# A first transfer to 16 partitions, and a later first store, in an RMSNorm with swish

## The chip, the core and the metric

The kernel runs on one core of one Trainium2 chip. Its metric is the device time of one execution in microseconds (us), as the median of a few runs.

## What is computed

`x` has 16 x 1024 rows of 512 fp32 values. Each row is divided by its root mean square, multiplied by `gamma`, and put through swish.

```python
rms = np.sqrt(np.mean(x ** 2, axis=-1, keepdims=True) + eps)
x_norm = x / rms * gamma
return (x_norm * (1.0 / (1.0 + np.exp(-x_norm)))).astype(np.float32)
```

So 33.55 MB are read from HBM and 33.55 MB are written to it, and each value is touched a handful of times in between.

## The kernel before

**Layout.** The 16,384 rows of `x` are cut into four groups of 4,096. In a group, partition p of SBUF holds 32 rows that lie one after another in memory (64 KB). A "row" below is one such row on all 128 partitions, 256 KB. The SBUF buffer `xb` is a ring of 96 rows: group 0 in rows 0 to 31, group 1 in 32 to 63, group 2 in 64 to 95, and group 3 again in 0 to 31 (`slots`, L29). Everything is done in place in `xb`.

**Loads** (`loads`, L30 to L32) are triples of group, first row and count, all issued by SyncE (SP) on one DMA queue, q1, in the order of the list: 4, 4, 8, 8 and 8 rows of group 0, 16 and 16 of group 1, 24 and 8 of group 2, 24 and 8 of group 3. Each one is a single DMA of 128 runs, one per partition. The first two (`early = 2`, L38) are moved into the preamble of the program. Only the loads of group 3 have to wait: they overwrite group 0, so SP waits (L127) until the stores of those rows have landed. Each load has a semaphore, `ld[i]`.

**Compute** goes in 18 chunks (`units`, L36): 4, 4, then 14 times 8, then 4 and 4 rows. For chunk k:

- `square(k)`, ScalarE (ACT): waits for the load that begins with this chunk (L166), then squares and sums some rows with an accumulator (L168), and squares the rest into `sq` (L176).
- `sums(k)`, VectorE (DVE): sums `sq` over the row (L225) and adds eps (L232).
- GpSimd (POOL) raises to the power -0.5 (L153).
- `norm(k)`, DVE: x times rstd times gamma, one instruction per row (L243).
- `swish(k)`, ACT: Silu over the chunk (L188), two chunks behind `square`.

`gamma` arrives by a small DMA on ACT's queue (L206), behind another small one (L202), and is spread to all partitions by one shuffle on DVE (L256), ahead of the first `norm`.

**Stores** (`stores`, L33 and L34) are issued by ACT on its own DMA queue, q10: 24 and 8 rows of group 0, 32 of group 1, 16 and 16 of group 2, and 16, 8, 8 of group 3. `hold` (L35) delays two of them: store 0 (24 rows of group 0) is issued at chunk 7 at the earliest, and ACT waits (L196) until the load of rows 0 to 23 of group 2 has landed; store 2 waits in the same way for rows 0 to 23 of group 3. ACT runs its instructions in order, so what stands behind such a wait waits with it. The order on ACT around store 0 is: `square(7)`, the wait for the load, store 0, store 1, `swish(5)`, `square(8)`, `swish(6)`.

At the end SP waits for the stores that it has not waited for yet (L265).

Of the kernel before, what the change touches and what calls it, by code (L numbers as in the profile page):

```python
# [9 lines left out]
def kernel(  # L10
# [7 lines left out]
    nc = tc.nc  # L18
    P = nc.NUM_PARTITIONS
# [4 lines left out]
    xf = x.flatten_outer_dims()  # L24
# [2 lines left out]

    groups = [32] * 4
    slots = [0, 32, 64, 0]  # L29
    loads = [(0, 0, 4), (0, 4, 4), (0, 8, 8), (0, 16, 8), (0, 24, 8)]  # L30
    loads += [(1, 0, 16), (1, 16, 16)]
    loads += [(2, 0, 24), (2, 24, 8), (3, 0, 24), (3, 24, 8)]  # L32
    stores = [(0, 0, 24), (0, 24, 8), (1, 0, 32), (2, 0, 16), (2, 16, 16)]  # L33
    stores += [(3, 0, 16), (3, 16, 8), (3, 24, 8)]  # L34
    hold = {0: (loads.index((2, 0, 24)), 7), 2: (loads.index((3, 0, 24)), 12)}  # L35
    behind = {}  # L36
    units = [4, 4] + [8] * 14 + [4, 4]
    ring = 96  # L38
    early = 2
# [3 lines left out]
    assert P * sum(groups) == R, R  # L43
    assert all(s + n <= ring for s, n in zip(slots, groups))

    chunks, row = [], 0
    for n in units:
        g = max(g for g in range(len(groups)) if first[g] <= row)
        r = row - first[g]
        i = next(i for i, (h, q, m) in enumerate(loads) if h == g and q <= r < q + m)  # L50
        assert r + n <= loads[i][1] + loads[i][2]
        chunks.append((slots[g] + r, row, n, i if r == loads[i][1] else None))
        row += n
    K = len(chunks)
    rows = row
    assert rows * P == R
# [29 lines left out]
    ld = [nc.alloc_semaphore(f"ld{t}") for t in range(len(loads))]  # L86
# [16 lines left out]
    def need(ins, sem, value):  # L103
        return ins.wait_op(sem, value, "sem-ge")

    def dram(ap, piece):
        g, r, n = piece
        rows = ap[P * first[g] : P * (first[g] + groups[g])]
        return rows.rearrange("(p n) d -> p n d", n=groups[g])[:, r : r + n, :]

    def place(piece):
        g, r, n = piece
        return slots[g] + r, slots[g] + r + n

    def buf(piece):
        a, b = place(piece)
        return xb[:, a:b, :]

    stored_by_sync = set()

    def load(i):
        a, b = place(loads[i])
        for u, piece in enumerate(stores):
            c, d = place(piece)
            over = piece[0] < loads[i][0] and c < b and a < d
            if (over or behind.get(i) == u) and u not in stored_by_sync:
                nc.sync.wait_ge(st[u], 16)  # L127
                stored_by_sync.add(u)
        return nc.sync.dma_start(
            out=buf(loads[i]), in_=dram(xf, loads[i])  # L130
        ).then_inc(ld[i], 16)

    entry = nc.main_func.blocks[0].instructions
# [1 line left out]
    for t in range(early):  # L135
        ins = load(t).ins
        assert here[-1] is ins or here[-1].name == ins.name
        here.pop()
        at = next(
            i for i, other in enumerate(entry)  # L140
            if other.engine == mybir.EngineType.SP
            and isinstance(other, mybir.InstDrain)
        )
        entry.insert(at, ins)
    for t in range(early, len(loads)):
        load(t)
# [4 lines left out]
    for k, (_, row, n, _) in enumerate(chunks):  # L151
        need(
            nc.gpsimd.tensor_tensor(  # L153
                out=rstd[:, row : row + n], in0=ms[:, row : row + n],
# [7 lines left out]
    def square(k):  # L162
        nonlocal n_acc
        at, row, n, landing = chunks[k]
        if landing is not None:
            nc.scalar.wait_ge(ld[landing], 16)  # L166
        for j in range(n_sq[n], n):
            acc = nc.scalar.activation(  # L168
                out=junk[n_acc % 2], in_=xb[:, at + j, :], func=AF.Square,
                scale=inv_d**0.5, accum_out=ms[:, row + j : row + j + 1],  # L170
            )
            if n_acc >= 2:
                need(acc, s_acc, n_acc - 1)
            acc.then_inc(s_acc, 1)
            n_acc += 1
        square = nc.scalar.activation(  # L176
            out=sq[k % 2][:, : n_sq[n], :], in_=xb[:, at : at + n_sq[n], :],
            func=AF.Square, scale=inv_d**0.5,
        )
        if k >= 2:  # L180
            need(square, s_sum, k - 1)
        square.then_inc(s_sq, 1)

    def swish(k):
        at, _, n, _ = chunks[k]
        block = xb[:, at : at + n, :]
        need(
            nc.scalar.activation(out=block, in_=block, func=AF.Silu), s_norm, k + 1  # L188
        ).then_inc(s_swish, 1)
# [20 lines left out]
    stored = 0  # L210
    for k in range(K + 3):
        if k < K:
            square(k)
        while stored < len(stores) and max(ends[stored] + 2, after(stored)) <= k:
            store(stored)
            stored += 1
        if 2 <= k < K + 2:
            swish(k - 2)
# [3 lines left out]
    def sums(k):  # L222
        _, row, n, _ = chunks[k]
        need(
            nc.vector.tensor_reduce(  # L225
                out=ms[:, row : row + n_sq[n]], in_=sq[k % 2][:, : n_sq[n], :],
                op=ALU.add, axis=mybir.AxisListType.X,
            ),
            s_sq, k + 1,
        ).then_inc(s_sum, 1)  # L230
        need(
            nc.vector.tensor_scalar(  # L232
                out=ms[:, row : row + n], in0=ms[:, row : row + n],
                scalar1=eps_f, scalar2=None, op0=ALU.add,
            ),
            s_sum, k + 1,
        ).then_inc(s_eps, 1)
# [12 lines left out]

    for k in range(K + 1):
        if k < K:
            sums(k)
# [47 lines left out]
```

## Time and profile before

| | |
|---|---|
| median of 3 runs | 160.8 us (160.52 to 160.92) |
| the profiled execution, its own time | 160.12 us |
| span of its trace | 158.8 us |
| DVE busy | 131.6 us, 83% of the span |
| ACT busy | 125.0 us, 79% |
| POOL busy | 35.1 us, 22% |
| moved by DMA | 67.14 MB, mean 423 GB/s |
| first square on ACT starts | 4.92 us |
| DVE gets gamma, shuffle starts | 13.06 us |
| stores 0 and 1 issued | from 56.53 us |
| last store issued | 146.25 us |

The profile describes one execution. Its own time is 1.32 us above the span of its trace, and 0.68 us below the median of the runs. Busy times of engines leave out the issuing of DMAs; the row DMA of the page gives the share of time in which the 16 DMA engines were busy, in 40 equal slices of the span.

### The profile page before, as it was taken

Reading aid. Unit: us, or ns where it says so; the run is one execution under the profiler, and the core shown is the slowest. Engines: PE = TensorE matmul, PEld = TensorE weight load, DVE = VectorE, ACT = ScalarE, POOL = GpSimd, SP = SyncE. Lnnn points to the kernel's source line nnn. Section 1 sums busy time; section 2 is a strip of 40 time slices with the busy share of each in tenths; the row PEclk is TensorE's granted clock in tenths of the full one; section 3 lists DMA queues with packets and bytes.
Section 4 is the critical chain, followed back from the end, with each engine's and each line's share of the span. In section 5 each row is a group of like instructions: output and inputs, shape, how many; then the busy total and the mean of one; then the engine's idle time right before and its main releaser. Section 6 shows DMA issues by size and latency. Waiting matters only on the chain.

```text
span 158.8 us, 403 instructions
## 1 busy us (share of the span) xinstructions
DVE 131.6 (83%) x167; ACT 125.0 (79%) x137; POOL 35.1 (22%) x24
## 2 busy tenths in 40 slices
DVE  0117989999999999999999999999999999993000
ACT  0949699499898979998989898989898939786000
POOL 1021152213040505050505050504031323030000
DMA  7999999999999799999999989989979999999997
GB/s 281 443 415 446 421 499 404 396 470 448 404 433 522 305 363 491 396 409 400 417 491 409 458 388 429 561 380 413 528 305 454 429 421 429 454 413 437 400 437 310
DMA packets 2890, 67.14 MB, mean 423 GB/s; under 512 B 452, under 2 KB 452, under 8 KB 456
## 3 DMA queue, kind: packets, MB, share of 16 engines
q1 hardware_dynamic: 1584, 33.56, 50.0%
q10 hardware_dynamic: 1304, 33.57, 49.0%
q14 instruction: 2, 0.02, 0.0%
HBM read 33.56 MB, written 33.56 MB: 423 GB/s over the span
## 4 chain that ended last, share of the span: by engine, by line
DVE 68%; ACT 11%; DMA 7%; issue 4%; ACTq 1%; POOL 0%; another core or an unknown queue 0%; POOLq 0%
DVE xb L243 45%; DVE ms L225 21%; DMA gamma<-in_gamma_dram 7%; ACT sq L176 4%; ACT junk L168 4%; ACT xb L188 4%; DVE ms L232 1%; ACTq L198 0%; DVE gamma_sb L256 0%; POOL gamma L150 0%; POOL blank L149 0%; ACTq L196 0%; POOLq L68 0%
## 5 line engine op out<-in xcount | busy, mean ns | idle before, releaser
L243 DVE SCALAR_TENSOR_TENSOR xb<-xb,rstd,gamma_sb 128x512 f32<-128x512 f32 x128 | 86.2, 746 | 0.0
L188 ACT ACTIVATE xb<-xb 128x4096 f32<-128x4096 f32 (+1 forms) x18 | 58.3, 3236 | 14.8 <-DVE xb L243 14.8
L153 POOL TENSOR_TENSOR rstd<-ms,neg_half 128x8 f32<-128x8 f32 (+1 forms) x18 | 34.3, 1907 | 103.7 <-DVE ms L232 103.7
L225 DVE TENSOR_REDUCE ms<-sq 128x5 f32<-128x2560 f32 (+1 forms) x18 | 44.3, 2462 | 5.7 <-ACT sq L176 5.6
L176 ACT ACTIVATE sq<-xb 128x2560 f32<-128x2560 f32 (+1 forms) x18 | 36.3, 2019 | 0.0
L168 ACT ACTIVATE junk<-xb 128x512 f32<-128x512 f32 x50 | 29.1, 581 | 2.8 <-DMA xb<-in_x_dram 2.6
L168 ACT ACTIVATION_READ_ACCUMULATOR junk<-xb 128x1 f32 x50 | 9.3, 186 | 0.0
L209 ACT ACT_TABLE_LOAD x1 | 1.3, 1283 | 3.6 <-issue 3.6
L256 DVE LOAD_MASK_SELECT gamma_sb<-gamma x1 | 0.0, 14 | 4.4 <-DMA gamma<-in_gamma_dram 4.4
L232 DVE TENSOR_SCALAR ms<-ms 128x8 f32<-128x8 f32 (+1 forms) x18 | 3.1, 171 | 0.6
L220 DVE MEMSET neg_half<- 128x8 f32 x1 | 0.1, 65 | 2.0 <-PEq L68 2.0
L256 DVE STREAM_SHUFFLE gamma_sb<-gamma 128x512 f32<-128x512 f32 x1 | 0.7, 719 | 0.0
L150 POOL MEMSET gamma<- 128x512 f32 x1 | 0.5, 524 | 0.0
L149 POOL MEMSET blank<- 128x16 f32 x1 | 0.1, 111 | 1.5 <-POOLq L68 1.5
L282 POOL MEMSET const-float32-0.0<- 128x1 f32 x1 | 0.1, 98 | 0.2 <-issue 0.2
L282 POOL MEMSET const-bfloat16-1.0<- 128x1 bf16 x1 | 0.1, 101 | 0.0
L282 POOL MEMSET const-uint8-127<- 128x1 uint8 x1 | 0.1, 101 | 0.0
L282 POOL MEMSET const-float32-1.0<- 128x1 f32 x1 | 0.1, 98 | 0.0
## 6 DMA issues: line engine op xcount, KB each, us to landing
xb<-in_x_dram SPq DMA_DIRECT2D x2, 6144.0 KB, 35.7
out_dram<-xb ACTq DMA_DIRECT2D x3, 4096.0 KB, 20.5
xb<-in_x_dram SPq DMA_DIRECT2D x5, 2048.0 KB, 19.1
xb<-in_x_dram SPq DMA_DIRECT2D x2, 4096.0 KB, 33.0
out_dram<-xb ACTq DMA_DIRECT2D x1, 6144.0 KB, 19.9
out_dram<-xb ACTq DMA_DIRECT2D x3, 2048.0 KB, 12.6
xb<-in_x_dram SPq DMA_DIRECT2D x2, 1024.0 KB, 5.6
scratch<-blank ACTq DMA_DIRECT2D x1, 8.0 KB, 9.7
```

Source lines behind the costliest of these rows:

```text
L149: nc.gpsimd.memset(blank, 0.0).then_inc(s_blank, 1)
L150: nc.gpsimd.memset(gamma4, 0.0).then_inc(s_zero, 1)
L153: nc.gpsimd.tensor_tensor(out=rstd[:, row : row + n], in0=ms[:, row : row + n], in1=neg_half[:, :n], op=ALU.pow,),
L168: acc = nc.scalar.activation(out=junk[n_acc % 2], in_=xb[:, at + j, :], func=AF.Square, scale=inv_d**0.5, accum_out=ms[:, row + j : row + ...
L176: square = nc.scalar.activation(out=sq[k % 2][:, : n_sq[n], :], in_=xb[:, at : at + n_sq[n], :], func=AF.Square, scale=inv_d**0.5,)
L188: nc.scalar.activation(out=block, in_=block, func=AF.Silu), s_norm, k + 1
L209: nc.scalar.preload_act_table_set("silu_and_others")
L225: nc.vector.tensor_reduce(out=ms[:, row : row + n_sq[n]], in_=sq[k % 2][:, : n_sq[n], :], op=ALU.add, axis=mybir.AxisListType.X,),
L232: nc.vector.tensor_scalar(out=ms[:, row : row + n], in0=ms[:, row : row + n], scalar1=eps_f, scalar2=None, op0=ALU.add,),
L243: ins = nc.vector.scalar_tensor_tensor(out=x_row, in0=x_row, scalar=rstd[:, row + j : row + j + 1], in1=gamma_sb, op0=ALU.mult, op1=ALU.mult,)
L256: nc.vector.stream_shuffle(gamma_sb, gamma4, [0] * 32), s_gld, 16
L282: nc = _bacc.Bacc("TRN2", target_bir_lowering=False, num_devices=1)
```

## The change

Two things change. First, the loads of rows 0 to 15 of group 0. Before, they were three DMAs over all 128 partitions (4, 4 and 8 rows). Now a new first DMA loads all 16 rows of partitions 0 to 15 (16 runs of 32 KB), and the three old ones leave those partitions out and carry partitions 16 to 127 (112 runs each). The two DMAs in the preamble are now the 16-partition one and the first of the three. A chunk may now need more than one load, so `chunks` holds a list and `square` waits for each load in it; the first chunk waits for two.

Second, group 2 is loaded as 27 and 5 rows (was 24 and 8), and store 0 waits for the 27. What is left to load when store 0 may go is then 5 rows (was 8).

The order of instructions on DVE, ACT and POOL is the same as before, apart from the added wait of ACT. SP issues 12 loads (were 11).

```diff
-    loads = [(0, 0, 4), (0, 4, 4), (0, 8, 8), (0, 16, 8), (0, 24, 8)]
-    loads += [(1, 0, 16), (1, 16, 16)]
-    loads += [(2, 0, 24), (2, 24, 8), (3, 0, 24), (3, 24, 8)]
+    loads = [(0, 0, 16), (0, 0, 4), (0, 4, 4), (0, 8, 8), (0, 16, 8), (0, 24, 8)]
+    loads += [(1, 0, 16), (1, 16, 16), (2, 0, 27), (2, 27, 5)]
+    loads += [(3, 0, 24), (3, 24, 8)]
...
-    hold = {0: (loads.index((2, 0, 24)), 7), 2: (loads.index((3, 0, 24)), 12)}
+    hold = {0: (loads.index((2, 0, 27)), 7), 2: (loads.index((3, 0, 24)), 12)}
     behind = {}
+    narrow = {0: (0, 16), 1: (16, P), 2: (16, P), 3: (16, P)}
...
+    parts = [(0, P)] * len(loads)
+    for i, p in narrow.items():
+        parts[i] = p
...
+        need_now = [
+            i for i, (h, q, m) in enumerate(loads)
+            if h == g and q < r + n and r < q + m and i not in awaited
+        ]
+        awaited.update(need_now)
+        chunks.append((slots[g] + r, row, n, need_now))
...
     def load(i):
+        p, q = parts[i]
...
-            out=buf(loads[i]), in_=dram(xf, loads[i])
+            out=buf(loads[i])[p:q], in_=dram(xf, loads[i])[p:q]
...
-        if landing is not None:
-            nc.scalar.wait_ge(ld[landing], 16)
+        for i in landing:
+            nc.scalar.wait_ge(ld[i], 16)
```

## The prediction

> **What bounds the kernel now.** I read the page first: the busy shares, the slices, the DMA queues.
>
> ```profile
> DVE 131.6 (83%) x167; ACT 125.0 (79%) x137; POOL 35.1 (22%) x24
> ...
> DMA  7999999999999799999999989989979999999997
> GB/s 281 443 415 446 421 499 404 396 470 448 404 433 522 305 363 491 396 409 400 417 491 409 458 388 429 561 380 413 528 305 454 429 421 429 454 413 437 400 437 310
> DMA packets 2890, 67.14 MB, mean 423 GB/s; under 512 B 452, under 2 KB 452, under 8 KB 456
> ...
> q1 hardware_dynamic: 1584, 33.56, 50.0%
> q10 hardware_dynamic: 1304, 33.57, 49.0%
> ```
>
> DVE has the largest busy share of the compute engines, and the chain of waits runs mostly through it. But it stops in slice 37 of 40, while DMA is full from the first slice to the last: loads (q1) and stores (q10) take 50.0% + 49.0% of 16 engines' time. The DMA engines are the bound. What lengthens their work, or idles them, is paid in full; what moves compute is free while stores are issued in time.
>
> The trace's packet records give the DMA sum. One run on one partition is one packet; 16 packets are in flight at any time, and a 128-run DMA gives each engine 8. A packet of 8 KB takes 309 ns, 16 KB 611, 32 KB 1,213, 48 KB 1,815, 64 KB 2,418. Per engine that is 16 x 0.309 + 64 x 0.611 + 40 x 1.213 + 24 x 1.815 + 8 x 2.418 = 155.5 us. The engines' first packets start at 1.01 to 1.52 us, and the last one ends at 158.4: some 1.7 us are lost on the way. The busy times by stretch show where.
>
> ```profile
> 1.00:4.00 3.00, 0.07 (x1) 0.38 (x1) 0.57 (x2) 1.00 0.96 371
> ...
> 55.00:57.00 2.00, 2.00 (x4) 1.28 (x1) 0.00 (x0) 1.00 1.02 434
> 57.00:60.40 3.40, 3.37 (x4) 2.99 (x1) 0.59 (x1) 1.00 1.03 308
> ...
> 95.00:99.00 4.00, 4.00 (x6) 3.42 (x4) 0.00 (x0) 1.00 1.01 430
> ```
>
> The last two numbers are DMA share and GB/s. The engines are "busy" from 57.0 to 60.4 us, yet move 308 GB/s, not 430: 3.40 x (1 - 308/430) = 0.96 us is lost, with 16 KB packets of up to 1.28 us. This lies between the issue of stores 0 and 1 (56.53 us) and their first packet (60.38 us in the records). Around store 2 (issued 95.89) nothing is lost. So there are two places to win, the start and this stretch, and the change touches both.
>
> **Part 1, rows 0 to 15.** Before, per engine: 8 x (0.309 + 0.309 + 0.611) = 9.83 us. After, if the packets are spread evenly and run at the speeds above: 1 x 1.213 + 7 x 1.229 = 9.81. One more DMA costs SP one issue (0.4 us, the rows of 0.00 and 0.42 us); SP has issued all it may by 5.42 us, and the next load's data are due tens of us later, so that is hidden. The first chunk waits for two loads, 1.4 MB instead of 1.0; that is also hidden, since DVE sits until 13.06 us for gamma and ACT for 2.62 us for the third load.
>
> What the trace doesn't show is a large DMA into 16 partitions only. All 16 packets of the new first DMA go there at once. Lower bound: each runs at the 32 KB row, 1.213 us. Upper bound: in the trace a partition never gets more, over a load, than its share, 430 / 128 = 3.36 GB/s; if 16 neighbours can't take more than 16 shares, 32,768 B / 3.36 = 9.75 us, with all engines behind them. The only small case, gamma's four packets of 2 KB (81 to 84 ns), were spread over partitions 0, 32, 64, 96 and did not meet. No row is near; I take the middle, 5.5 us: **+4.3 us** (ends 0 and +8.5). For the three 112-run DMAs the bounds are 7 x 1.229 = 8.60 (engines) and 9.83 (as slow as with 128 partitions); I take 9.2: **+0.6** (ends 0 and +1.2).
>
> The Trainium skill (SBUF — State Buffer, "Door 1: The DMA port swizzle") speaks against the change: a DMA reaches memory through 16 ports, partitions 0 to 15 lie behind four of them, and 1 MiB to these partitions was measured at 104 GB/s. By that figure 512 KB would take an estimated 5.0 us, 3.8 above the packet row instead of my 4.3, and the sum below would give 164.6 us. By the packet row alone it would cost nothing. No run shown here has such a transfer, and the records of before can't decide: their 16 streams are spread over all 128 partitions.
>
> At the start there is something to gain: engines begin over 0.51 us (1.01 to 1.52), and first packets of 8 KB take up to 0.71 us. With 16 runs to describe instead of 128 all could begin together. Between 0 and 0.5 I take **-0.25**.
>
> **Part 2, store 0 waits for 27 rows.** A row takes 8 x 1.815 / 24 = 0.605 us, so the awaited load lands 3 x 0.605 = 1.8 us later. The timeline around the wait:
>
> ```profile
> 53.96 2.32 ACT L176 ACTIVATE sq<-xb 128x2560 f32<-128x2560 f32 x1
> 56.53 0.83 ACTq L198 DMA_DIRECT2D out_dram<-xb  x2
> ...
> 57.41 3.62 ACT L188 ACTIVATE xb<-xb 128x4096 f32<-128x4096 f32 x1 [1.13 <-DVE xb L243]
> ...
> 62.77 2.28 ACT L176 ACTIVATE sq<-xb 128x2560 f32<-128x2560 f32 x1
> ...
> 65.08 2.83 DVE L225 TENSOR_REDUCE ms<-sq 128x5 f32<-128x2560 f32 x1
> ```
>
> ACT is done at 56.28 and now waits only some 0.2 us. After, it waits about 1.8 us longer, with stores 0 and 1, `swish(5)` and `square(8)` queued behind. DVE's L225 starts within 0.03 us of the end of that square, so DVE, busy to the end from here, moves 1.8 us too. The stores it feeds are early enough: store 5 is issued at 134.71 and its first packet runs at 139.01, store 7 at 146.25 and 153.5. Cost **0** in this part; if that cover is gone, 1.3 us (rival D).
>
> DMA: with 5 rows left, 5 x 0.605 = 3.0 us of loads remain, less some 0.4 between last packet and landing. A store needs at least the 1.01 us that the first load took from issue to packet, so q1 still covers it. The gain lies in the slow stretch: none if it has nothing to do with the stores (as around store 2), all 0.96 if it is their issue beside many loads. I take a third, **-0.3**, since one of two such places shows it and 5 of 8 rows remain.
>
> **Sum.** +4.3 + 0.6 - 0.25 - 0.3 = +4.35. On the profiled execution: 160.12 + 4.35 = 164.5. The median of the runs lies 0.68 higher, so **165.1 us**. Compute goes along: if the loads come 4.6 us later and ACT's wait another 1.8, the last store is issued at about 152.5, and its turn on the engines comes at 153.5 + 4.35 = 157.9.
>
> **The rivals.**
> A, the forecast, 0.61: the 16 partitions can't take 16 streams at full speed. For: no row shows a partition range taking more than its share. Own range: from packets at half speed, 2.4 us (+1.2 - 0.55, 161.5) to all ends at once (9.7 - 0.25, 170.3).
> B, 0.27, not slower: the engines alone limit, as every packet row has it (27 GB/s per engine whatever the size). Then part 1 is -0.25 and part 2 about half of 0.96, together -0.75: 160.05, with 159.3 (both gains in full) to 160.6. It decides if the first 32 KB packets take under 1.5 us.
> C, 0.07: the spread is not what the change wants: the 16 packets go to the few engines that otherwise serve these partitions. Then those take 9.8 us for it and skip the next three DMAs, and each engine's total is as before: 160.8, 160.4 to 161.1. The first chunk would start after 10 us, hidden by gamma.
> D, 0.05: the start is like B, but the moved compute reaches the DMA. Store 5 would be issued at 136.5. If the 3.5 to 3.9 us from issue to first packet (stores 2 and 0) are needed in a busy queue too, its data start at 140.2, while store 4 is drained at about 138.8: +1.3 after the gains, 161.9. It decides if a store's first packet comes over 3 us after its issue with its queue empty.
>
> The Trainium skill (DMA: Bandwidth & Descriptors, "Why a DMA increments its semaphore by 16 and not by 1") speaks against C: the number of engines is the largest up to 16 that divides the outer sizes, and both 16 and 112 give 16. Nothing in the trace shows it for these shapes.
>
> **How the numbers follow.** About 0.3% (0.5 us) is what can be told from no change here. A and D are slower: 0.66. C and the upper end of B (0.03) are within 0.3%: 0.10. The rest of B is faster: 0.24. The range starts at 160.0, which leaves out the lower half of B (0.13), and ends at 169.5, which leaves out the last of A (0.04); A alone is 161.5 to 170.3.
>
> **What would show it.** Right: from 1 to 6 us the DMA moves 110 to 250 GB/s while "busy", the first packets are 32 KB of 3 us or more, and ACT's first square starts at 8 us or later (4.92 before); the awaited load lands past 62 us. Wrong: 420 GB/s from the second us on, 32 KB packets of 1.2 us. For part 2: ACT idle for some 1.8 us ahead of store 0, and GB/s between store 0's issue and its first packet; 430 there means the stretch was curable, 308 that it moved along. An idle slice of DMA near 139 us would speak for D.

## The result and the profile after

The changed kernel takes 168.42 us (median of 5, 167.50 to 168.74) against 160.69 us of the kernel before in the same comparison (160.05 to 160.92): a ratio of 1.0477, 95% interval 1.045 to 1.0504, so 7.7 us slower. The forecast was 165.1 us, slower. The profiled execution took 168.42 us with a span of 167.1.

The page of the changed kernel, the lines that answer to those of before:

```profile
DVE 131.7 (79%) x167; ACT 124.9 (75%) x137; POOL 35.1 (21%) x24
...
DMA  8899999998999997999899899999998999999995
GB/s 127 192 310 304 318 435 451 400 478 377 480 480 452 437 424 308 447 529 400 357 510 388 376 447 392 463 455 392 424 471 361 431 424 431 447 416 447 400 435 255
DMA packets 2874, 67.14 MB, mean 402 GB/s; under 512 B 468, under 2 KB 468, under 8 KB 472
```

The compute engines do the same work, and the DMA engines are still busy: the row DMA stands at 7 to 9 in every slice but the last. But in the first five slices (20.9 us) the row GB/s stands at 127 to 318 where it stood at 281 to 446. "Busy" is not "moving": the time is lost inside the packets. The busy times by stretch set a border to it. The last column is GB/s; the bytes of a packet are counted where it starts. First the kernel before:

```profile
4.00:8.00 4.00, 0.80 (x1) 3.87 (x9) 0.00 (x0) 1.00 1.06 440
8.00:12.00 4.00, 0.59 (x2) 1.56 (x4) 1.01 (x1) 1.00 1.00 424
12.00:16.00 4.00, 2.91 (x6) 3.82 (x7) 0.84 (x1) 1.00 1.01 434
```

Then the changed kernel:

```profile
1.00:4.00 3.00, 0.07 (x1) 0.39 (x1) 0.57 (x2) 1.00 1.20 175
4.00:8.00 4.00, 0.00 (x0) 0.89 (x1) 0.00 (x0) 1.00 0.85 184
8.00:12.00 4.00, 0.00 (x0) 1.92 (x5) 0.00 (x0) 1.00 1.03 293
12.00:16.00 4.00, 1.77 (x4) 2.60 (x6) 1.01 (x1) 1.00 1.06 310
16.00:20.00 4.00, 3.96 (x7) 0.00 (x0) 1.47 (x1) 1.00 0.93 274
20.00:57.00 37.00, 32.76 (x38) 33.29 (x40) 8.28 (x4) 1.00 1.03 444
57.00:60.40 3.40, 3.37 (x7) 3.40 (x8) 2.07 (x1) 1.00 1.02 439
60.40:64.00 3.60, 3.60 (x6) 2.19 (x1) 0.00 (x0) 1.00 0.78 338
64.00:68.00 4.00, 3.97 (x6) 1.19 (x1) 1.88 (x1) 1.00 1.17 497
```

Where 424 to 440 GB/s stood from 4 to 16 us, there are 184 to 310. The loss ends at 20 us, when rows 0 to 15 have landed (19.94 us). Everything behind comes later than before, so the place to look for the slow stretch of before is not 57.0 to 60.4 us, but ahead of this kernel's own first store, which is issued at 65.94 us and has its first packet at 67.36. The last two lines make 422 GB/s together, and the packet records show 0.04 us lost there: the stretch is gone.

The packet records give the terms. "Undisturbed" is the time that a packet of its size takes almost everywhere else in the traces, as listed in the prediction. Per engine, rows 0 to 15 took 10.12 us before. After, the one packet of 32 KB took 3.61 us on the mean (3.00 to 3.99, undisturbed 1.213), the 14 packets of 8 KB 7.13 us in all (0.510 each, undisturbed 0.309) and the 7 of 16 KB 6.50 us (0.928 each, undisturbed 0.611): 17.24, which is **7.1 us more**. The following load lost another 0.3.

ACT saw it at once. The timeline of the changed kernel, where the first square and the first store are issued:

```profile
10.08 0.60 ACT L178 ACTIVATE junk<-xb 128x512 f32<-128x512 f32 x1 [5.19 <-DMA xb<-in_x_dram]
...
60.27 2.32 ACT L186 ACTIVATE sq<-xb 128x2560 f32<-128x2560 f32 x1
65.94 0.82 ACTq L208 DMA_DIRECT2D out_dram<-xb  x2
66.81 3.62 ACT L198 ACTIVATE xb<-xb 128x4096 f32<-128x4096 f32 x1 [4.22 <-DMA xb<-in_x_dram]
```

The first square starts at 10.08 us (4.92 before). ACT is done at 62.59 and stands still until the 27 rows have landed and store 0 goes, at 65.94.

### The profile page after: what moved, and what is told of

The parts are those of the page before. It is cut to its first block, busy times and chain, and to the rows that moved or that the text cites. A ratio compares the mean times of both kernels' runs of the same rounds, so it can differ in the third digit from the quotient of the medians.

```text
span 167.1 us, 405 instructions
## 1 busy us (share of the span) xinstructions
DVE 131.7 (79%) x167; ACT 124.9 (75%) x137; POOL 35.1 (21%) x24
## 4 chain that ended last, share of the span: by engine, by line
DVE 62%; ACT 13%; DMA 11%; issue 3%; another core or an unknown queue 2%; ACTq 0%; SPq 0%
DVE xb L253 41%; DVE ms L235 20%; DMA xb<-in_x_dram 11%; ACT sq L186 5%; ACT junk L178 5%; ACT xb L198 4%; DVE ms L242 1%; ACTq L208 0%; SPq L139 0%; ACTq L206 0%; ACTq L176 0%
## 6 DMA issues: line engine op xcount, KB each, us to landing
out_dram<-xb ACTq DMA_DIRECT2D x3, 4096.0 KB, 19.4
xb<-in_x_dram SPq DMA_DIRECT2D x1, 6144.0 KB, 19.4
```

## Experiments

The theory after this: the loads of rows 0 to 15 cost 7 us because of the set of partitions they go to, and the wait for 27 rows is free. The rivals: the wait is paid by what stands behind it on ACT; the start of a program or the memory side, not the partitions, makes the first DMA slow.

### Each part by itself

Part 1 alone:

```diff
-    loads += [(1, 0, 16), (1, 16, 16), (2, 0, 27), (2, 27, 5)]
+    loads += [(1, 0, 16), (1, 16, 16), (2, 0, 24), (2, 24, 8)]
...
-    hold = {0: (loads.index((2, 0, 27)), 7), 2: (loads.index((3, 0, 24)), 12)}
+    hold = {0: (loads.index((2, 0, 24)), 7), 2: (loads.index((3, 0, 24)), 12)}
```

> Part 1 alone: the 16-partition DMA and the three 112-run DMAs, with 24 + 8 rows of group 2 and the old wait. Theory (all of the loss comes from the loads of rows 0 to 15): 168.4 us like the whole change, or up to 1 us more if the wait for 27 rows had won something; rows 0 to 15 are in at 19.9 us instead of 11.7. Rival (part of the loss is the wait for 27 rows, 1.8 us): 166.5 us.

Measured: 166.82 us, ratio 1.0406 (1.0369 to 1.0444) against 160.35 us of before. Rows 0 to 15 are in at 19.4 us, half a us earlier than in the whole change. So part 1 is 6.5 us of the 7.7, and about 1.2 us is left for part 2. The theory had 168.4; the rival's 166.5 is nearer.

Part 2 alone:

```diff
-    loads = [(0, 0, 16), (0, 0, 4), (0, 4, 4), (0, 8, 8), (0, 16, 8), (0, 24, 8)]
+    loads = [(0, 0, 4), (0, 4, 4), (0, 8, 8), (0, 16, 8), (0, 24, 8)]
...
-    narrow = {0: (0, 16), 1: (16, P), 2: (16, P), 3: (16, P)}
+    narrow = {}
```

> Part 2 alone: rows 0 to 15 are loaded by the three 128-run DMAs as before; group 2 is loaded as 27 + 5 rows and store 0 waits for the 27. Theory (all of the loss comes from the loads of rows 0 to 15): not slower than before; 0 to -0.96 us, the latter if the slow stretch of 3.4 us at 308 GB/s ahead of the first store is gone, as it is in the trace of the changed kernel (439 GB/s from 57.0 to 60.4, and the first store packet 1.4 us after its issue instead of 3.9). Rival (the longer wait of ACT is paid): +1.3 to +1.8 us. About 160.1 against 162.2 us.

Measured: 161.20 us, ratio 1.0046 (1.0025 to 1.0067). Part 2 costs 0.74 us. (The expectation compares the same clock times, 57.0 to 60.4 us, in two kernels that are 7 us apart there; the place is the one ahead of the first store, as said above.) "Not slower" falls; but it is less than the 1.3 to 1.8 of the rival too. The two parts together make 4.5% of the 4.8%.

### Which set of partitions, alone on the engines

These are twelve extra loads, each alone on the engines, ahead of the kernel before, whose own loads then no longer go in the preamble (eight of the twelve left out here):

```diff
-    early = 2
+    early = 0
...
+    tried = [
+        (16, slice(0, 16), slice(0, 16)),
+        (16, slice(0, 128, 8), slice(0, 128, 8)),
+        (16, slice(0, 16), slice(0, 128, 8)),
+        (16, slice(0, 128, 8), slice(0, 16)),
...
+    for t, (n, to, of_) in enumerate(tried):
+        nc.sync.dma_start(
+            out=xb[to, 0:n, :], in_=dram(xf, (0, 0, n))[of_]
+        ).then_inc(s_try, 16)
+        nc.sync.wait_ge(s_try, 16 * (t + 1))
```

> The kernel before with no load in the preamble and twelve extra loads ahead of its own, each waiting until the one ahead of it has landed, into rows that are loaded again afterwards. 16 runs of 32 KB: (1) partitions 0-15; (2) every 8th partition; (3) into 0-15, from the memory rows of every 8th; (4) into every 8th, from the memory rows of 0-15; (5) every 7th; (6) 112-127; then 32 KB runs to (7) partitions 0-31 and (8) 0-63; then 16 KB runs to (9) 16-127, (10) 0-111, (11) 0-127, (12) 0-95. Theory (the way into neighbouring partitions is shared): packets of (1), (3) and (6) take 3 to 5 us, those of (2) and (4) half of that or less, those of (5) near 1.2 us; (7) takes as long per packet as (2), (8) twice (7) in all. For (9) and (10): packets of 0.7 to 1.1 us if the uneven spread of 112 partitions is what slowed the three DMAs, 0.61 if they were slowed by what the 16-partition DMA left behind. Rival R1 (the memory side: neighbouring rows of x): (1) and (4) are slow, (2) and (3) fast. Rival R2 (the first DMA of a program, or few long runs, are slow wherever they go): all 16-run DMAs are alike, or only (1) is slow.

Measured, in the busy times by stretch of this kernel, one line for each of the twelve loads in their order (it took 250.26 us as a whole, with these loads in front):

```profile
2.40:6.90 4.50, 0.00 (x0) 1.28 (x1) 0.00 (x0) 1.00 0.90 120
9.50:12.40 2.90, 0.00 (x0) 0.00 (x0) 0.00 (x0) 1.00 0.80 181
14.10:18.80 4.70, 0.00 (x0) 0.00 (x0) 0.00 (x0) 1.00 0.78 112
21.20:24.30 3.10, 0.00 (x0) 0.00 (x0) 0.00 (x0) 1.00 0.71 169
26.00:29.10 3.10, 0.00 (x0) 0.00 (x0) 0.00 (x0) 1.00 0.70 169
30.40:34.90 4.50, 0.00 (x0) 0.00 (x0) 0.00 (x0) 1.00 0.84 117
37.00:42.60 5.60, 0.00 (x0) 0.00 (x0) 0.00 (x0) 1.00 0.87 187
44.70:55.30 10.60, 0.00 (x0) 0.00 (x0) 0.00 (x0) 1.00 0.93 195
56.90:64.00 7.10, 0.00 (x0) 0.00 (x0) 0.00 (x0) 1.00 0.93 258
65.70:72.90 7.20, 0.00 (x0) 0.00 (x0) 0.00 (x0) 1.00 0.95 255
74.70:80.70 6.00, 0.00 (x0) 0.00 (x0) 0.00 (x0) 1.00 0.90 350
81.90:89.50 7.60, 0.00 (x0) 0.00 (x0) 0.00 (x0) 1.00 0.91 207
```

The reader is to see three things in the last column.

The destination decides. Lines 1 and 3 write partitions 0 to 15, from different rows of memory: 120 and 112 GB/s. Lines 2 and 4 write every eighth partition, line 4 from the very rows that line 1 read: 181 and 169. So R1, the memory side, falls, and R2 as well: lines 2 and 4 have 16 runs too and are faster, and line 6 (112 to 127) comes late and is as slow as line 1.

It is a matter of which partitions, not only of how many. 16 partitions far apart take more than 16 neighbours; 64 neighbours (195) take hardly more than 32 (187). Every seventh partition was expected at full speed and came no faster than every eighth.

And 112 partitions don't give 112/128 of the rate of 128: lines 9 and 10 stand at 258 and 255 where 350 x 112/128 would be 306, and 96 partitions (207) are worse still. Their 16 KB packets took 0.94 and 0.97 us on the mean, alone on the engines, as against 0.68 for 128 partitions. That is the slowness of the 16 KB packets of the third 112-run load in the changed kernel (0.928), so it has this of itself and not from the 16-run DMA ahead. For the two with 8 KB packets this was not run alone. There the first 16 packets, which start while 32 KB packets are still in flight (to 5.57 us), took 1.13 us on the mean, and the later ones mostly 0.4 to 0.6: some 0.8 us per engine may belong to the 16-run DMA.

The Trainium skill (SBUF — State Buffer, "Door 1: The DMA port swizzle") has 104, 189 and 196 GB/s for 1 MiB to partitions 0 to 15, 0 to 31 and 0 to 63, and says that bits of the partition number pick one of 16 ports; the lines above agree (112 to 120, 187 and 195), and every eighth partition reaches eight ports by its formula, like 0 to 31. By the formula 112 and 96 partitions both reach all 16 ports; here the measurement decides, 255 to 258 and 207 GB/s against 350. Why these two are slow is not shown: the records don't name engines or ports.

### Part 1 with one size changed

The split at partition 32 instead of 16 (this run and the next have 24 + 8 rows of group 2 and the old wait, as in part 1 alone):

```diff
-    narrow = {0: (0, 16), 1: (16, P), 2: (16, P), 3: (16, P)}
+    narrow = {0: (0, 32), 1: (32, P), 2: (32, P), 3: (32, P)}
```

> Part 1 with one size changed: the first DMA takes partitions 0 to 31 (32 runs of 32 KB), the next three the other 96. Theory (each DMA goes at the rate that its set of partitions had when loaded by itself: 0-31 188 GB/s, 96 partitions 208 GB/s): 1.05 MB in 5.6 us and 3.15 MB in 15.1 us, 20.7 in all, against 4.5 + 14.0 = 18.5 with 16 and 112 partitions; so about 2.2 us slower than part 1 alone, 169 us. Rival (only the narrow first DMA is costly, and 32 partitions are twice as wide): 1.5 to 2.5 us faster than part 1 alone, 165 us.

Measured: 167.35 us, ratio 1.0435 (1.0399 to 1.0470). That is not faster than part 1 alone, and 0.5 us slower, which the two intervals leave open: the wider first DMA is repaid by slower 96-partition loads (16 KB packets of 1.09 us). The sum of the single rates, 169, was too dark; a rate measured alone includes the time in which a DMA starts and ends with some engines empty (the DMA share in the twelve lines is 0.70 to 0.95).

Rows 0 to 3 alone:

```diff
-    loads = [(0, 0, 16), (0, 0, 4), (0, 4, 4), (0, 8, 8), (0, 16, 8), (0, 24, 8)]
+    loads = [(0, 0, 4), (0, 0, 4), (0, 4, 4), (0, 8, 8), (0, 16, 8), (0, 24, 8)]
...
-    narrow = {0: (0, 16), 1: (16, P), 2: (16, P), 3: (16, P)}
+    narrow = {0: (0, 16), 1: (16, P)}
```

> Part 1 for rows 0 to 3 alone: the first DMA loads 4 rows of partitions 0 to 15 (16 runs of 8 KB), the second these rows of the other 112; rows 4 to 15 come over 128 partitions as before. Theory (own rates: 117 and 262 GB/s): 1.1 + 3.5 = 4.6 us instead of 2.5 to 2.8, so about +2 us, 162.4. Rival (a short first DMA lets the engines start together, and only its size made it dear): -0.3 to +0.3 us, 160.4.

Measured: 161.02 us, ratio 1.0044 (1.0017 to 1.0071): slower, by 0.7 us instead of 2. The 256 packets of 8 KB took 6.73 us per engine instead of 5.2 to 5.5, so 1.3 to 1.5 us of loss, while the time grew by half of that. (The slow stretch ahead of store 0 is not there in this kernel, see the table below.) A short first DMA wins nothing at the start either: the 16 first packets start at 1.01 to 1.43 us, in the changed kernel at 1.00 to 1.84, in the kernel before at 1.01 to 1.52 and, in a second execution, at 0.99 to 1.62.

### The slow stretch, and the price of the later store

The kernel before, once more:

> The kernel before once more, for its trace: is the slow stretch between the issue of store 0 (56.5 us) and its first packet (60.4 us) there again? If it belongs to the issue of two stores beside eight rows of loads, there are again some 3 us with 16 KB packets of over 1 us. If it was a disturbance of that one execution, all 16 KB packets there take 611 ns, and the span is about 1 us shorter.

Measured: 161.63 us in this one execution. The stretch is there again, weaker: 16 KB packets of up to 1.14 us. Summing over all packets what they took above their undisturbed time, and dividing by 16, shows how much each engine lost at the three places where the work changes between loads and stores. "First" is around the first packet of store 0 (60 us), "second" around the first packet of the load of group 3 (80 us), "third" around the first packet of store 2 (99 us); in us per engine, from the packet records of one execution each. "End" is how long an engine on the mean stood without a packet before the last packet of the execution had ended:

| kernel | store 0 waits for | first | second | third | end | ratio to before |
|---|---|---|---|---|---|---|
| before | 24 rows | 1.06 | 0.02 | 0.03 | 0.4 | |
| before, second execution | 24 | 0.31 | 0.25 | 0.04 | 2.3 | |
| ACT busier (below) | 24 | 0.69 | 0.02 | 0.08 | 0.4 | 0.9998 (0.9982 to 1.0014) |
| 24 + 3 + 5 rows, wait for 24 | 24 | 0.81 | 0.02 | 0.01 | 0.9 | 0.9995 (0.9982 to 1.0008) |
| 20 + 12 rows | 20 | 0.96 | 0.02 | 0.02 | 1.2 | 1.0006 (0.9992 to 1.0021) |
| 26 + 6 rows | 26 | 0.28 | 0.14 | 0.07 | 1.5 | 1.0039 (1.0015 to 1.0063) |
| part 2 alone | 27 | 0.04 | 0.62 | 0.79 | 0.9 | 1.0046 (1.0025 to 1.0067) |
| 24 + 3 + 5 rows, wait for 27 | 27 | 0.06 | 0.62 | 0.75 | 1.0 | 1.0054 (1.0035 to 1.0073) |
| 28 + 4 rows | 28 | 0.04 | 0.69 | 0.03 | 0.1 | 1.0026 (1.0010 to 1.0041) |
| part 1 alone | 24 | 0.03 | 0.05 | 0.03 | 0.8 | 1.0406 (1.0369 to 1.0444) |
| part 1, rows 0 to 3 | 24 | 0.04 | 0.06 | 0.10 | 0.8 | 1.0044 (1.0017 to 1.0071) |
| part 1, split at 32 | 24 | 0.04 | 0.05 | 0.05 | 0.8 | 1.0435 (1.0399 to 1.0470) |
| the whole change | 27 | 0.04 | 0.54 | 0.71 | 1.0 | 1.0477 (1.045 to 1.0504) |

The losses are means over the engines, but a kernel ends with its last packet. The second execution of the kernel before lost less in slow packets than the first and still took 1.5 us longer: from 158.4 to 159.9 us only one packet at a time was in flight, and its last stretch reads

```profile
157.00:160.30 3.30, 0.00 (x0) 0.00 (x0) 0.00 (x0) 1.00 0.11 45
```

So the table says where packets were slow. What a change costs is to be read from the ratios, which stand on many runs.

The second execution of the kernel before also showed that ACT's short wait in the first is not the rule: ACT is done with `square(7)` at 54.99 us there and waits 2.0 us, not 0.2, before store 0 goes. Its timeline, and below it that of part 2 alone:

```profile
52.66 2.33 ACT L176 ACTIVATE sq<-xb 128x2560 f32<-128x2560 f32 x1
56.95 0.82 ACTq L198 DMA_DIRECT2D out_dram<-xb  x2
57.83 3.62 ACT L188 ACTIVATE xb<-xb 128x4096 f32<-128x4096 f32 x1 [2.84 <-DMA xb<-in_x_dram]
```

```profile
52.61 2.32 ACT L186 ACTIVATE sq<-xb 128x2560 f32<-128x2560 f32 x1
58.47 0.82 ACTq L208 DMA_DIRECT2D out_dram<-xb  x2
59.34 3.62 ACT L198 ACTIVATE xb<-xb 128x4096 f32<-128x4096 f32 x1 [4.41 <-DMA xb<-in_x_dram]
```

Store 0 goes 1.5 us later (1.9 against the first execution). Is that paid by the compute behind it on ACT? The same shift without any change of DMA, three unused squares behind stores 0 and 1:

```diff
+    waste = sbuf("waste", [P, 3])
...
             store(stored)
             stored += 1
+            if stored == 2:
+                for w in range(3):
+                    need(
+                        nc.scalar.activation(
+                            out=junk[n_acc % 2], in_=xb[:, chunks[k + 1][0], :],
+                            func=AF.Square, accum_out=waste[:, w : w + 1],
+                        ),
+                        s_acc, n_acc - 1,
+                    ).then_inc(s_acc, 1)
+                    n_acc += 1
```

> The kernel before with three more squares on ACT (1.85 us, results unused) right after stores 0 and 1 are issued: what stands behind on ACT, and so DVE and stores 2 to 7, move by about the 1.9 us that the wait for 27 rows costs, but loads and stores 0 and 1 are as before. Theory T1 (the moved compute is paid): 161.2. Theory T2 (compute has slack; part 2 costs by what the DMA does at the change from loads to stores): 160.4, with the last store issued at 148 us and its packets starting as soon as the store ahead is done.

Measured: 160.29 us, ratio 0.9998. T2 holds. In this kernel's timeline, stores 5 to 7 are issued at

```profile
136.66 0.34 ACTq L199 DMA_DIRECT2D out_dram<-xb  x1
...
143.30 0.34 ACTq L199 DMA_DIRECT2D out_dram<-xb  x1
...
148.21 0.34 ACTq L199 DMA_DIRECT2D out_dram<-xb  x1
```

the same times as in part 2 alone to 0.03 us, and it costs nothing. So part 2 is not paid through ACT or DVE. Nor is it the shape of the last loads (here and in the runs that follow, rows 0 to 15 are loaded as before):

```diff
-    loads += [(1, 0, 16), (1, 16, 16), (2, 0, 27), (2, 27, 5)]
+    loads += [(1, 0, 16), (1, 16, 16), (2, 0, 24), (2, 24, 3), (2, 27, 5)]
...
-    hold = {0: (loads.index((2, 0, 27)), 7), 2: (loads.index((3, 0, 24)), 12)}
+    hold = {0: (loads.index((2, 0, 24)), 7), 2: (loads.index((3, 0, 24)), 12)}
```

> The kernel before with rows 24 to 31 of group 2 loaded as 3 + 5 rows, so that five rows come last in packets of 10 KB as in the changed kernel, but store 0 waits for 24 rows as before. If the later store (ACT's longer wait, or what it moves) is what costs 0.8 us in part 2: as before, 160.4. If the shape of the last loads is: 161.2.

Measured: 160.26 us, as before. With the same loads and the wait on the 3 rows instead (`loads.index((2, 24, 3))`):

> Group 2 loaded as 24 + 3 + 5 rows, and store 0 waits for the 3: the wait for 27 rows without the 27-row DMA. The trace of part 2 alone has its slow 16 KB packets at the two later changes, from the stores of group 0 to the load of group 3 (74 to 90 us, 0.63 us per engine) and on to store 2 (94 to 104 us, 0.79 us), where the kernels with a wait for 24 rows have 0.02 to 0.26 and 0.01 to 0.11. Theory T3 (the later issue of store 0 causes it): slow like part 2 alone, 161.2, with these stretches. Rival (the packets of 54 KB or the one large DMA cause it): as before, 160.3.

Measured: 161.38 us, and the slow packets at the second and third place, like part 2 alone. T3 holds for 27 rows: the later issue of store 0 costs 0.7 to 0.9 us by the ratios, with one load of 27 rows or with 24 and 3. And the dose, with `(2, 0, n), (2, n, 32 - n)` and the wait on the first of them:

> Group 2 as 20 + 12 rows, store 0 waits for the 20 (1.2 us of loads earlier than in chunk 7's order it can go at all, so about 54 to 55 us). T3 (a later issue costs, an earlier one doesn't): as before, 160.3, within 0.3. Rival (24 rows are a point of balance, each side costs): 160.8 or more.

> Group 2 as 26 + 6 rows, store 0 waits for the 26. If the cost grows with the wait: 160.3 + 2/3 of 0.8 = 160.9. If it sets in at a point: 160.3 or 161.2.

> Group 2 as 28 + 4 rows, store 0 waits for the 28. If the cost grows with the wait: 161.5. Rival (it is a matter of how the engines happen to stand to each other at the later changes): anything between 160.2 and 161.5, with the slow packets at other changes than in part 2 alone. Four rows are 2.4 us of loads and the first store packet came 1.4 us after its issue in part 2 alone, so no engine idles ahead of the first store.

Measured: 160.49, 161.03 and 160.83 us. An earlier store costs nothing; 26, 27 and 28 rows all cost 0.26% to 0.54%, with intervals that overlap, and not in the order of the wait. The intervals allow no choice between "grows" and "sets in". With 28 rows the third place is quiet, the second is not.

For 26 and 28 rows the slow packets can't be the whole price: at the three places together they lost 0.5 and 0.8 us, no more than the 0.6 to 1.1 of the kernels that wait for 24 rows or fewer with the old loads in front (27 rows: 1.4). The profiled execution with 26 rows has its loss at the end (1.5 us). With 28 rows the moved compute does reach the DMA. ACT goes on 1.8 us later than with 27 (61.16 instead of 59.34), store 5 is issued at 138.45, and the packets ahead of it end at 137.8 to 139.0 (a line of its timeline, and one of its busy times by stretch):

```profile
138.45 0.34 ACTq L208 DMA_DIRECT2D out_dram<-xb  x1
...
138.00:139.00 1.00, 1.00 (x3) 1.00 (x4) 0.00 (x0) 1.00 0.01 0
```

No data packet starts between 138 and 139 us, the first of store 5 at 139.29; each engine stood idle for 0.94 us on the mean, and in return they finish almost together (0.1). That is the idle slice that the prediction named as the sign of D, in a kernel that waits one row longer.

## Why the prediction was right, and where its sizes were off

- **The bound.** Right in the main: of the 8.3 us between the two profiled executions (168.42 and 160.12), 7.8 are longer packets. The rest is idle time at the end, where the engines finish apart (1.0 us on the mean, 0.4 before), which the prediction had left out.
- **The 16-run DMA, +4.3 us (0 to +8.5).** The mechanism held: 16 neighbouring partitions don't take 16 streams. The size was too large: 3.61 - 1.21 = **+2.4 us** per engine, or some 0.8 more with the first 8 KB packets behind it, which are counted in the next term.
- **The 112-run DMAs, +0.6 us (0 to +1.2).** The mis-sized term. Measured 7.13 + 6.50 - 8.60 = **+5.0 us**. The upper bound took for granted that a DMA to 112 partitions takes at most as long as one to 128; loaded alone it takes longer, 1.8 MB at 258 GB/s against 2.1 MB at 350.
- **The start, -0.25 us.** Nothing of it was seen. The first packets of 16 runs start over 0.84 us in the changed kernel and over 0.42 to 0.66 in the two others with a 16-run DMA, against 0.51 and 0.63 with 128 runs. Fewer runs didn't bring the engines together.
- **The wait for 27 rows, -0.3 us.** The stretch before the first store went, as hoped, but packets as slow came up at the two later changes: -1.0 and +1.2 us against the profiled execution, **+0.74 us** in the runs of part 2 alone. Part 1 alone took the first stretch away too, with the old wait, so in the whole change it can't be booked to part 2.
- **The cover.** ACT's longer wait is free, as priced: 1.9 us of added work on ACT cost 0.0 us. But the cover is thinner than it was read: 139.01 us is where the last engine starts store 5 before, the first one does at 138.12, and with 28 rows the cover was gone. That ACT waited only 0.2 us was not so in the second execution of the kernel before (2.0).
- **The rivals.** B falls with the 32 KB packets of 3.0 to 4.0 us. C falls too: all 16 packets of 32 KB were in flight at once from 1.84 to 4.0 us and done at 5.57, where a few engines would have needed 9.8 us. D: no engine waited for store 5 in the changed kernel. With 28 rows the engines did, but not for D's reason: with the queue empty, store 5's first packet came 0.84 us after its issue, not 3.
- The terms as measured on the engines: +2.4 + 5.0 - 1.0 + 1.2, and 0.3 in the load that follows, make +7.9, less some 0.3 that the first packets of before lost as well: +7.6. With 0.6 more idle time at the end that is 8.2, against 8.3 between the two profiled executions and 7.7 in the runs. The sum of the prediction was too small by 3.3 us, and its share for the 16-run DMA too large. That the two errors in part 1 had opposite signs (some 1.9 us too much, 4.4 too little) and the range was 9.5 us wide helped the forecast: the direction came from its mechanism, how near the number came is in part luck.

What stays open: why the packets of one queue double in time shortly before the other queue's first packet, and why the later issue of store 0 moves that from the first place to the second and third. What is shown is where it lies, and that with 27 rows the issue time decides; by which way the later store is paid with 26 rows is open. A slow start took the stretch away from the first place without bringing it up at the others (the three variants of part 1 in the table), so the order of the engines among themselves may matter; that is a guess. The stretch that is gone would account for part 1's loss of 7 us costing 6.5, and that of the rows-0-to-3 variant, 1.3 to 1.5, only 0.7; this too was not tested. No kernel beat the one before.

## What to carry to other kernels

Where DMA is the bound, a transfer that leaves out some partitions is dear on both sides: the piece cut off is slow, and the rest is slower than its share, so a cut at partition 16 cost 6.5 us on 4 MB. Read GB/s and not the busy share of DMA, and compare the time of single packets with their undisturbed time: that tells a slow transfer from an idle engine. Look also at how far apart the engines finish, since the last one sets the time. A slow stretch that goes away at one place has to be looked for at the next before it is booked as a gain.

## What the runs showed of the hardware that was not expected

- 96 partitions loaded alone run at 207 GB/s, hardly above 64 (195) or 32 (187); 112 at 255 to 258; 128 at 350, for 16 KB runs at 96, 112 and 128 and 32 KB runs at 32 and 64.
- A 16-run DMA doesn't start its engines more closely together than a 128-run DMA: 0.42 to 0.84 us from first to last, against 0.51 and 0.63.
- At a change between loads and stores many packets of the queue that goes out take about twice their time, single ones up to three times, 0.3 to 1.1 us lost per engine in one place.
- The first packet of store 0 came the later after its issue the more rows were still to load: 4.5 us with 12 rows, 3.0 to 3.9 with 8, 2.3 with 6, 1.4 with 5 and 0.9 with 4. It doesn't go by the size of the packets ahead: with 8 rows loaded as 3 + 5 it was 3.8.
- The engines of one DMA-bound kernel can finish 2.8 us apart in one execution and 0.9 in another, and the time of the kernel goes with the last.
